# The second matrix products of both MLPs by two-by-two blocks in seven products, over pairs of chunks

## The chip, the cores and the metric

The program runs on one core of one Trainium2 chip. The time is the time on the device, in microseconds (us), from the start to the end of one execution; the kernel before took 1902.31 us (median of three runs, 1901.79 to 1906.84). Engines are named as in the profile: PE is the matrix engine, PEld its weight loads, DVE the vector engine, ACT the scalar engine, POOL the GpSimd engine, SP the engine that issues most DMAs.

## The reference, cut to what matters

The model is two trunk layers on 256 context tokens and 512 latent tokens of width 1024. Layer 0 mixes with differential attention, layer 1 with neighbourhood attention; behind each stands a dense MLP with a gate. Only the MLPs change here:

```
def squared_relu_mlp(h, w1, w2):
    return jnp.square(jax.nn.relu(h @ w1)) @ w2          # 1024 -> 4096 -> 1024
...
x = x + gate * squared_relu_mlp(modulate(rms_norm(x, g), shift, scale), w1, w2)
```

In layer 0 the MLP works on all 768 tokens, in layer 1 on the 512 latent tokens alone. Inputs and output are float32.

## The kernel before, in words

**Precision.** Every large product is made from float32 operands that are split in two: a rounded part, which ACT copies out as fp32r, and the rest, which POOL (weights, line 146) or DVE (activations) gets by subtraction. A product is then three matmuls (`PASSES`, line 59: high by high, high by low, low by high). So each weight tile of 128 by 1024 costs one ACT copy (line 145) and one POOL subtraction (line 146), and each PE product is threefold.

**The MLP** (`mlp`, line 810) goes over 16 chunks of 256 hidden units. `up(c)` makes the hidden chunk: two groups of weights are loaded and split, PE multiplies (line 830) into the PSUM tiles `D0` and `D1`, ACT takes the ReLU (lines 835 and 838), DVE squares (line 839), ACT and DVE split the result (lines 841 and 842) into tiles of tag `H`. `down` (line 856) multiplies a chunk with its two rows of `w2`: for each tile of 128 tokens and each half of 512 output columns six matmuls (line 865; two hidden halves, three passes) fill one PSUM tile, and DVE adds it to an accumulator in SBUF (line 876). The PSUM tile has the tag `A` for the left half and `B` for the right one; each tag has two buffers, so four groups of six can be in flight. `up` of the next chunk is issued ahead of `down` of this one. The last two chunks go through `down` together, straight onto the residual: before that `blend` (line 847) multiplies the accumulators by the gate (line 853, DVE) and adds them to the residual `xh` (line 854, POOL for the left, DVE for the right half), and then each PSUM tile is multiplied by the gate and added too (lines 871 and 872). In layer 0, `done0` passes each pair of finished token tiles on to the normalisation for layer 1.

**Buffers.** Raw weights land in `R` (two buffers), split weights in `W` (four buffers). The accumulators of layer 0 take four tiles `H`; the residual sits in `E` and `X` during the whole MLP.

**Order.** In the MLPs nothing is ordered by hand: a scheduler that builds the program fixes each engine's order ahead of time, and each engine then runs its own list in order, waiting on semaphores. Between the chunks of layer 0, `side` issues work for layer 1: a modulation chunk (line 257 on PE) and tables of position bias (line 594 on POOL).

## Time and profile before

| | |
|---|---|
| median of three runs | 1902.31 us |
| the profiled execution | 1902.15 us, of which the span from first to last instruction is 1899.6 us |
| granted clock of PE, mean over the span | 0.981 |
| PE busy | 1786.5 us (94%) |
| DVE busy | 1133.4 us (60%) |
| POOL busy | 812.6 us (43%) |
| MLP of layer 0 in the span | from about 550 to about 1138 us |
| MLP of layer 1 in the span | from about 1541 us to the end |

The page of the profile shows one execution. A busy PE is not PE at its peak, since matmuls are pipelined; how long a matmul takes in a row of matmuls is read from the distance of starts. In the time lines, an instruction of DVE or POOL that waits for access to the memory is shown as busy, not as idle: its duration grows.

### The profile page before, as it was taken

The numbers are of one execution on the slowest core, as the hardware profiler recorded it, in microseconds if no ns is written. First come the engines' busy times: TensorE is split into PE (matmuls) and PEld (weight loads), VectorE is DVE, ScalarE is ACT, GpSimd is POOL, SyncE is SP. The second block draws the span as 40 slices with busy tenths as digits, with TensorE's granted clock in tenths as the row PEclk, the third lists the DMA queues.
The fourth block names the chain that finished last, engine by engine and source line by source line (L and its number), as shares of the span: only waits on it lengthen the run. The fifth ranks groups of instructions, "written<-read, shape, count | busy, mean of one in ns | idle before, by whom it ended". The sixth has DMA issues, their size and how long they took to land.

```text
span 1899.6 us, 27132 instructions
## 1 busy us (share of the span) xinstructions
PE 1786.5 (94%) x10256; PEld 1563.8 (82%) x10256; DVE 1133.4 (60%) x2158; ACT 833.7 (44%) x1854; POOL 812.6 (43%) x688
## 2 busy tenths in 40 slices
PE   6989999996999999999999998999998989999998
PEld 5878888884789888888888977989897778888886
DVE  4588777885574343343334676777777664444446
ACT  4476767774342212221221245777676342323321
POOL 3755566653224333342432432433345444444443
PEclk9999999997999999999999998999999999999999
DMA  8122222224324443443432132122212323223232
GB/s 329 42 84 78 87 87 87 79 71 169 119 73 136 132 160 111 167 162 116 148 134 85 56 100 64 57 71 74 65 67 89 117 92 97 89 91 109 90 101 76
DMA packets 66499, 197.61 MB, mean 104 GB/s; under 512 B 8192, under 2 KB 23488, under 8 KB 60224
## 3 DMA queue, kind: packets, MB, share of 16 engines
q1 hardware_dynamic: 58608, 186.03, 29.4%
q10 hardware_dynamic: 7760, 9.85, 1.5%
q8 instruction: 80, 1.31, 0.3%
q14 instruction: 51, 0.42, 0.1%
HBM read 180.74 MB, written 15.11 MB: 103 GB/s over the span
## 4 chain that ended last, share of the span: by engine, by line
PE 75%; DVE 11%; ACT 6%; issue 4%; POOL 2%; DMA 2%; ACTq 0%; SPq 0%; POOLq 0%; DVEq 0%
PE PD L830 22%; PE PA L408 14%; PE PA L865 11%; PE PB L865 9%; PE PA L750 4%; PE PA L257 2%; PE PS L517 2%; PE PB L552 2%; PE PQ L398 1%; PE PS L656 1%; PE PB L701 1%; PE PB L541 1%; PE PB L686 1%; DVE Y L423 1%; ACT W L145 1%
## 5 line engine op out<-in xcount | busy, mean ns | idle before, releaser
L146 POOL TENSOR_TENSOR W<-R,W 128x1024 fp32r<-128x1024 f32 x142 | 351.3, 2485 | 540.6 <-ACT W L145 537.0
L830 PE MATMUL PD<-Q,W 128*128 128x384 f32 (+2 forms) x1992 | 396.0, 346 | 2.4 <-DVE Q L334 1.1
L830 PEld LDWEIGHTS PD<-Q,W 128*128 128x128 f32 x1992 | 345.7, 188 | 33.7 <-issue 8.6
L145 ACT ACTIVATE W<-R 128x1024 fp32r<-128x1024 f32 (+1 forms) x172 | 172.7, 1021 | 450.7 <-PE PA L865 193.6
L865 PE MATMUL PA<-W,H 128*128 128x512 f32 x1080 | 275.4, 393 | 4.6 <-POOL W L146 3.0
L865 PEld LDWEIGHTS PA<-W,H 128*128 128x128 f32 x1080 | 200.1, 188 | 51.3 <-issue 4.5
L839 DVE TENSOR_TENSOR N<-N 128x768 f32<-128x768 f32 (+1 forms) x64 | 66.9, 1046 | 279.2 <-ACT N L835 170.4
L865 PE MATMUL PB<-W,H 128*128 128x512 f32 x840 | 209.2, 391 | 0.0
L865 PEld LDWEIGHTS PB<-W,H 128*128 128x128 f32 x840 | 157.4, 188 | 33.4
L408 PE MATMUL PA<-W,Q 128*128 128x384 f32 (+1 forms) x1008 | 174.3, 325 | 0.4 <-DVE H L621 0.4
L408 PEld LDWEIGHTS PA<-W,Q 128*128 128x128 f32 x1008 | 158.6, 191 | 0.7 <-DVE H L621 0.7
L296 POOL TENSOR_TENSOR SQ<-SQ,half 128x4 f32<-128x4 f32 (+1 forms) x96 | 94.7, 988 | 128.9 <-DVE SQ L421 127.7
L842 DVE SCALAR_TENSOR_TENSOR H<-N,H 128x768 fp32r<-128x768 f32 (+1 forms) x64 | 97.9, 1532 | 25.7 <-ACT H L841 25.0
L408 PE MATMUL PA<-WB,H 128*128 128x384 f32 x576 | 110.9, 345 | 0.8 <-DVE Q L469 0.8
L750 PE MATMUL PA<-W,H 128*128 128x512 f32 x384 | 97.5, 404 | 7.9 <-ACT H L743 5.1
L408 PEld LDWEIGHTS PA<-WB,H 128*128 128x128 f32 x576 | 101.1, 192 | 1.8 <-DVE Q L469 1.1
L830 PE MATMUL PD<-H,W 128*128 128x512 f32 (+1 forms) x408 | 94.1, 378 | 2.4 <-DVE SA L290 2.0
L876 DVE TENSOR_TENSOR H<-PA,H 128x512 f32<-128x512 f32 x78 | 53.8, 690 | 69.7 <-PE PA L865 69.7
L750 PEld LDWEIGHTS PA<-W,H 128*128 128x128 f32 x384 | 71.9, 192 | 25.9 <-ACT H L743 5.4
L523 ACT ACTIVATE E<-PS,SA 128x768 f32<-128x768 f32 (+1 forms) x96 | 72.9, 760 | 36.5 <-DVE SA L522 33.6
L830 PEld LDWEIGHTS PD<-H,W 128*128 128x128 f32 x408 | 73.8, 188 | 18.0 <-DVE H L334 2.9
L517 PE MATMUL PS<-Q,Q 128*128 128x256 f32 (+1 forms) x320 | 70.2, 352 | 19.1 <-ACT Q L446 9.9
(210 smaller groups left out, 3052.6 us busy)
## 6 DMA issues: line engine op xcount, KB each, us to landing
R<-in_w_dram SPq DMA_DIRECT2D x128, 512.0 KB
M<-in_wmod_dram SPq DMA_DIRECT2D x48, 1024.0 KB
R<-in_wqa_dram SPq DMA_DIRECT2D x32, 384.0 KB
R<-in_wqb_dram SPq DMA_DIRECT2D x32, 384.0 KB
Y<-in_rpb_dram SPq DMA_DIRECT2D x48, 128.0 KB
bias<-Y SPq DMA_DIRECT2D x48, 128.0 KB
X<-bias SPq DMA_DIRECT2D x8, 768.0 KB
R<-in_woa_dram SPq DMA_DIRECT2D x8, 512.0 KB
```

The costliest lines, as they stand in the source:

```text
L145: high = nc.scalar.activation(w[:, 0, :n], raw, AF.Copy)
L146: low = (eng or nc.gpsimd).tensor_sub(w[:, 1, :n], raw, w[:, 0, :n].bitcast(F32))
L296: nc.gpsimd.tensor_tensor(r, ss, self.half[:, :n], op=ALU.pow)
L408: nc.tensor.matmul(acc[:, :n], hT[kt][:, x, P * i:P * i + P], w[kt // 2][:, y, o:o + n], start=(kt == 0 and p == 0), stop=(kt == KT - 1 an ...
L517: nc.tensor.matmul(s[:, c0:c1], q[:, m, P * i:P * i + P], k[:, m, c0:c1], start=p == 0, stop=p == 1)
L523: nc.scalar.activation(e[:, m, :nk], s, AF.Exp, bias=mx[:, 0:1], accum_out=sm[:, m:m + 1])
L750: nc.tensor.matmul(ps, oHL[h][:, x, c:c + P], w[h // 2][:, y, 512 * (h % 2):512 * (h % 2) + 512], start=(first and h == hs[0] and p == 0), ...
L830: nc.tensor.matmul(ps[:, at:at + b1 - b0], w[kt // 4][:, x, o:o + P], hT[kt][:, y, b0:b1], start=(kt == 0 and p == 0), stop=(kt == KT - 1 ...
L839: nc.vector.tensor_mul(r, r, r)
L842: nc.vector.scalar_tensor_tensor(u[:, 1, :], r, 1.0, u[:, 0, :].bitcast(F32), op0=ALU.mult, op1=ALU.subtract)
L865: nc.tensor.matmul(ps, hd[:, x, P * i - c0:P * i - c0 + P], w[f][:, y, 512 * n:512 * n + 512], start=(f == 0 and p == 0), stop=(f == len(h ...
L876: nc.vector.tensor_add(av, ps, av)
```

## The change

`mlp` gets two new arguments. With `blocks`, chunks 0 to 13 are taken in seven pairs. The two chunks of a pair and the two halves of the output columns cut `w2` into four blocks of 256 by 512 (B11, B12, B21, B22; first index the chunk, second the column half), and the two halves of the tokens cut the hidden values into four blocks. The eight block products of a pair become seven, each of a sum or difference of hidden blocks with a sum or difference of weight blocks (Strassen's scheme in Winograd's form). Since one intermediate sum enters three of the four results, there are five accumulators (`C11`, `C12`, `C21`, `C22`, `U`), and `blend` adds `U` to the last three once at the end. Chunks 14 and 15 go as before. Eight block products in one pair were 144 matmuls in layer 0 and 96 in layer 1; the seven are 126 and 84.

In detail:

- `raw_hidden` keeps the hidden values in float32, unsplit; ACT now squares them (it was DVE). The subtractions and additions of hidden blocks run on DVE, and `split` then splits each of the seven sums (ACT copy, DVE subtraction).
- `block` loads a weight block (128 by 2 by 512). Sums of blocks run on DVE, in place, 1024 elements per partition; each of the seven is split like any weight (ACT, POOL). The four blocks of a pair are loaded seven times in all, since `products_a` (two products) and `products_b` (five) load their own.
- `product` takes one PSUM tile for each tile of tokens and adds it to one or two accumulators. It sets the tag of the tile by a counter's parity; the counter moves by two for each tile, so all tiles of a product have the same tag.
- The order of a pair is: `up` of the pair's second chunk, two products, `up` of the next pair's first chunk, five products. The last pair has no next chunk.
- In layer 0 the fifth accumulator and the float32 hidden values take the tiles `E` and `X`. So the residual is written to DRAM (`x1`, twelve DMAs on the ACT queue) before the MLP, and read back in `blend`; the gates are loaded there too. Raw weight blocks land in the four buffers `N` in layer 0, and in layer 1 in `R`, which has four buffers there, shared with the raw weights of `up`.

The diff, cut to its core:

```
@@ mlp
-    def mlp(self, l, t0, xh, hT, tag, mid, done, side):
+    def mlp(self, l, t0, xh, hT, tag, mid, done, side, blocks=None, spilled=None):
...
+            if blocks:
+                nc.scalar.activation(r, r, AF.Square)
+            else:
+                nc.vector.tensor_mul(r, r, r)
+        def parts(u, src):
+            nc.scalar.activation(u[:, 0], src, AF.Copy)
+            nc.vector.scalar_tensor_tensor(u[:, 1], src, 1.0, u[:, 0].bitcast(F32), op0=ALU.mult, op1=ALU.subtract)
...
+        def raw_hidden(c):
+            r = self.sbt(r_tags[c % 3], [P, 2, ntok])
+            for f, ps in up(c):
+                relu2(c, ps, r[:, f, :])
+            return [r[:, :, 128 * nh * t:128 * nh * t + 128 * nh] for t in range(2)]
+        def block(c, n):
+            raw = self.sbt(b_tag, [P, 1024])
+            self.last["SP"] = nc.sync.dma_start(
+                raw.rearrange("p (f n) -> p f n", f=2),
+                a["w2"][l, 2 * c:2 * c + 2, :, 512 * n:512 * n + 512].rearrange("f p n -> p f n"))
+            return raw
...
+        def product(u, w, *sums):
+            for i in range(nh):
+                self.n += 1
+                ps = self.pst('AB'[self.n % 2])
+                for f in range(2):
+                    for p, (x, y) in enumerate(PASSES):
+                        nc.tensor.matmul(ps, u[:, x, f, P * i:P * i + P], w[:, y, 512 * f:512 * f + 512],
+                                         start=(f == 0 and p == 0), stop=(f == 1 and p == 2))
+                for q, sign in sums:
+                    av = piece(q * nh + i)
...
+                    elif sign > 0:
+                        nc.vector.tensor_add(av, ps, av)
+                    else:
+                        nc.vector.tensor_sub(av, av, ps)
+        def products_a(c, r1):
+            b11, b22, b12 = block(c, 0), block(c + 1, 1), block(c, 1)
+            w, u = self.wsplit(b11, 1024), split(r1[0])
+            nc.vector.tensor_sub(b22, b22, b12)
+            product(u, w, (C11, 1), (U, 1))
+            nc.vector.tensor_sub(r1[0], r1[0], r1[1])
+            w, u = self.wsplit(b22, 1024), split(r1[0])
+            product(u, w, (C21, 1), (C22, 1))
+        def products_b(c, r1, r2):
+            b22, b11, b21, b12 = block(c + 1, 1), block(c, 0), block(c + 1, 0), block(c, 1)
+            w, u = self.wsplit(b21, 1024), split(r2[0])
+            product(u, w, (C11, 1))
+            nc.vector.tensor_sub(b12, b12, b11)
+            nc.vector.tensor_add(r1[1], r1[1], r2[1])
+            w, u = self.wsplit(b12, 1024), split(r1[1])
+            product(u, w, (C12, 1), (C22, 1))
+            nc.vector.tensor_sub(b11, b22, b12)
+            nc.vector.tensor_sub(r1[0], r2[1], r1[0])
+            w, u = self.wsplit(b11, 1024), split(r1[0])
+            product(u, w, (U, 1))
+            nc.vector.tensor_sub(r1[1], r2[0], r1[0])
+            w, u = self.wsplit(b22, 1024), split(r1[1])
+            product(u, w, (C12, 1))
+            nc.vector.tensor_sub(b12, b11, b21)
+            w, u = self.wsplit(b12, 1024), split(r2[1])
+            product(u, w, (C21, -1))
         def blend():
+            if spilled is not None:
+                gate.update(self.load_gates(l, 1, (0, 1) if t0 == 0 else (0,)))
+                xu = [self.sbt('EX'[j % 2], [P, 3, 512]) for j in range((nx + 2) // 3)]
+                for j in range(nx):
+                    i, n = t0 + j // 2, j % 2
+                    xh[i, n] = xu[j // 3][:, j % 3, :]
+                    nc.sync.dma_start(xh[i, n], spilled[i][:, 512 * n:512 * n + 512])
...
+                        if t or n:
+                            nc.vector.tensor_add(av, piece(U * nh + k), av)
@@ mlp, the loop
+            r1 = raw_hidden(0)
+            for c in range(0, nc_ - 2, 2):
+                r2 = raw_hidden(c + 1)
+                side()
+                products_a(c, r1)
+                side()
+                if c + 2 < nc_ - 2:
+                    nxt = raw_hidden(c + 2)
+                side()
+                products_b(c, r1, r2)
+                side()
+                r1 = nxt
+            hid = hidden(nc_ - 2)
@@ project, end
+                if l == 0:
+                    for n in range(2):
+                        nc.scalar.dma_start(self.x1[i][:, 512 * n:512 * n + 512], xh[i, n])
@@ hybrid_block
-            b.mlp(0, 0, xh, hT2, 'HH', mid0, done0, sideB)
+            b.mlp(0, 0, xh, hT2, 'HH', mid0, done0, sideB, ('HHHHE', 'XEX', 'N'), b.x1)
...
+        b.open("right", R=2)
...
-            b.mlp(1, 2, xh1, hT3, 'QH', lambda: None, done1, lambda: None)
+            b.mlp(1, 2, xh1, hT3, 'QH', lambda: None, done1, lambda: None, ('QQQQ', 'NNN', 'R'))
```

In what follows the seven products of a pair are called a1, a2 and b1 to b5, in the order of the code, and the six matmuls that fill one PSUM tile a group. Line numbers from 843 on in rows of the change are those of the changed file: L843 is `up`, L903 the matmul of `product`, L911 and L913 its additions, L861 the splitting of a hidden block, L919 to L942 the sums of blocks, L964 and L965 `blend`.

**PE in the MLP of layer 0.** Before, a stretch of `down` (line 865; tiles `PA` and `PB`) with pieces of `up` (line 830) between:

```order
L830 MATMUL PD_8776<-Q_6233,W_8768 128x384
L865 MATMUL PB_8686<-W_8638,H_8276 128x512 x3
L865 MATMUL PB_8686<-W_8643,H_8331 128x512 x3
L865 MATMUL PB_8702<-W_8638,H_8276 128x512 x3
L865 MATMUL PB_8702<-W_8643,H_8331 128x512 x3
L865 MATMUL PA_8678<-W_8638,H_8276 128x512 x3
L865 MATMUL PA_8678<-W_8643,H_8331 128x512 x3
L830 MATMUL PD_8776<-Q_6233,W_8768 128x384 x2
L830 MATMUL PD_8776<-Q_6234,W_8768 128x384 x2
L865 MATMUL PA_8694<-W_8638,H_8276 128x512 x3
```

Now, the products b1, b2 and the start of b3 in a pair:

```order
L903 MATMUL PA_7790<-W_7784,H_7787 128x512 x6
L273 MATMUL PA_7750<-sel,T_7759 128x2 x2
L903 MATMUL PA_7798<-W_7784,H_7787 128x512 x6
L903 MATMUL PA_7806<-W_7784,H_7787 128x512 x6
L903 MATMUL PA_7822<-W_7816,H_7819 128x512 x6
L903 MATMUL PA_7831<-W_7816,H_7819 128x512 x6
L903 MATMUL PA_7840<-W_7816,H_7819 128x512 x6
L843 MATMUL PD_7980<-Q_6232,W_7972 128x384 x2
L843 MATMUL PD_8031<-Q_6232,W_7972 128x384 x2
L903 MATMUL PA_7857<-W_7851,H_7854 128x512 x6
L903 MATMUL PA_7865<-W_7851,H_7854 128x512 x6
```

Six groups stand one behind the other with nothing between them but two small matmuls, and all use the tag `A`; before, both tags were in use at once and `up` filled in between.

**DVE at the same kind of place.** Before, the additions of one chunk with what stands among them:

```order
L839 TENSOR_TENSOR N_9988<-N_9988 128x768
L876 TENSOR_TENSOR H_6662<-PA_10030,H_6662 128x512
L842 SCALAR_TENSOR_TENSOR H_9991<-N_9988,H_9991 128x768
L876 TENSOR_TENSOR H_6662<-PB_10038,H_6662 128x512
L876 TENSOR_TENSOR H_6663<-PB_10054,H_6663 128x512
L267 TENSOR_TENSOR T_10006<-PA_9994,T_10006 2x256
L876 TENSOR_TENSOR H_6662<-PA_10046,H_6662 128x512
L876 TENSOR_TENSOR H_6663<-PB_10070,H_6663 128x512
```

Now, from the last addition of b1 to the first of b3 (another pair than above, with the tag `B`):

```order
L911 TENSOR_TENSOR H_6675<-PB_8942,H_6675 128x512
L911 TENSOR_TENSOR H_6676<-PB_8958,H_6676 128x512
L911 TENSOR_TENSOR H_6678<-PB_8958,H_6678 128x512
L280 TENSOR_TENSOR mB<-PA_8888,bT 128x4
L861 SCALAR_TENSOR_TENSOR H_9052<-E_8540,H_9052 128x768
L911 TENSOR_TENSOR H_6676<-PB_8967,H_6676 128x512
L911 TENSOR_TENSOR H_6678<-PB_8967,H_6678 128x512
L919 TENSOR_TENSOR N_9244<-N_9244,N_9246 128x1024
L911 TENSOR_TENSOR H_6676<-PB_8976,H_6676 128x512
L911 TENSOR_TENSOR H_6678<-PB_8976,H_6678 128x512
L861 SCALAR_TENSOR_TENSOR H_9251<-X_8775,H_9251 128x768
L911 TENSOR_TENSOR E_6679<-PB_8993,E_6679 128x512
```

Between the additions that free the PSUM tiles of b2 and b3 there now stand operations with both inputs in SBUF (L861 and L919), one between each two groups.

**POOL at the end of layer 0's MLP.** Before, the additions of `blend` (line 854) stand ahead of and among the last four splits of `w2`:

```order
L854 TENSOR_TENSOR E_6167<-E_6167,H_6662 128x512 x2
L854 TENSOR_TENSOR X_6168<-X_6168,H_6663 128x512
L854 TENSOR_TENSOR E_6169<-E_6169,H_6664 128x512 x2
L146 TENSOR_TENSOR W_10754<-R_10752,W_10754 128x1024
L854 TENSOR_TENSOR X_6170<-X_6170,H_6665 128x512
L146 TENSOR_TENSOR W_10759<-R_10757,W_10759 128x1024
L146 TENSOR_TENSOR W_10764<-R_10762,W_10764 128x1024
L146 TENSOR_TENSOR W_10769<-R_10767,W_10769 128x1024
L146 TENSOR_TENSOR H_10772<-R_10773,H_10772 128x768
```

Now (L965 is `blend`):

```order
L146 TENSOR_TENSOR W_10898<-R_10896,W_10898 128x1024
L146 TENSOR_TENSOR W_10903<-R_10901,W_10903 128x1024
L146 TENSOR_TENSOR W_10908<-R_10906,W_10908 128x1024
L146 TENSOR_TENSOR W_10913<-R_10911,W_10913 128x1024
L965 TENSOR_TENSOR X_10848<-X_10848,H_6675 128x512
L965 TENSOR_TENSOR E_10849<-E_10849,H_6677 128x512 x2
L965 TENSOR_TENSOR X_10850<-X_10850,H_6677 128x512
L965 TENSOR_TENSOR E_10847<-E_10847,H_6675 128x512
L146 TENSOR_TENSOR H_10916<-R_10917,H_10916 128x768
L965 TENSOR_TENSOR E_10847<-E_10847,H_6675 128x512
```

All six additions of `blend` on POOL have moved behind the last split of `w2`, and those for the first tokens (`E_10847`) are the last of them.

78 lines of the change are left out of this document (50 added, 28 removed).

## The prediction

> **What bounds the kernel now.** I read the page's first part, then the busy times by stretches of time, then the chain of waits and the groups of the two MLPs, then the time lines of single periods.
>
> ```profile
> span 1899.6 us, 27132 instructions
> PE 1786.5 (94%) x10256; PEld 1563.8 (82%) x10256; DVE 1133.4 (60%) x2158; ACT 833.7 (44%) x1854; POOL 812.6 (43%) x688
> ...
> 438.00:550.00 112.00, 96.75 (x470) 75.77 (x471) 68.13 (x124) 41.66 (x96) 29.90 (x21) 0.90 0.31 103
> 640.00:1045.00 405.00, 405.00 (x2257) 348.91 (x2256) 155.08 (x206) 87.66 (x109) 143.35 (x84) 1.00 0.39 134
> 1595.00:1836.00 241.00, 241.00 (x1055) 197.69 (x1054) 109.47 (x132) 69.60 (x88) 105.21 (x44) 1.00 0.31 96
> ...
> 645.95 2.63 PE PD L830 x15
> 682.63 2.63 PE PD L830 x15
> ...
> 1595.12 9.90 PE PD L830 x43
> 1617.09 9.90 PE PD L830 x43
> ```
>
> In the steady part of both MLPs (640 to 1045 and 1595 to 1836 us; the columns behind the length are PE, PEld, DVE, ACT, POOL, the granted clock, the DMA share and GB/s) PE is busy without a break at clock 1.00, and the chain repeats every 36.68 us in layer 0 and 21.97 us in layer 1, one period for each chunk. DVE is busy for 38% and 45% there. So PE bounds the MLPs, and a matmul taken away is worth its place in the row. A chunk of layer 1 is 96 matmuls of 512 columns: 21.97 / 96 = 0.2288 us each, 1.37 us for a group of six.
>
> **What PE saves.** In layer 0 a pair drops from 144 to 126 matmuls of 512 columns, in layer 1 from 96 to 84. Seven pairs each: 126 × 0.2288 = 28.8 us and 84 × 0.2288 = 19.2 us, together **−48.0 us**. A pair would take 2 × 36.68 − 4.12 = 69.2 us in layer 0 and 43.93 − 2.75 = 41.2 us in layer 1.
>
> **What the other engines get.** The rows of layer 0, then pieces of time lines from both layers:
>
> ```profile
> L146 POOL TENSOR_TENSOR W<-R,W 128x1024 fp32r<-128x1024 f32 x44 | 108.5, 2478 | 260.5 <-ACT W L145 260.5
> L876 DVE TENSOR_TENSOR H<-PA,H 128x512 f32<-128x512 f32 x67 | 46.3, 691 | 65.0 <-PE PA L865 65.0
> L145 ACT ACTIVATE W<-R 128x1024 fp32r<-128x1024 f32 x44 | 45.4, 1055 | 238.4 <-PE PA L865 193.6 <-PE PD L830 44.8
> L842 DVE SCALAR_TENSOR_TENSOR H<-N,H 128x768 fp32r<-128x768 f32 x22 | 34.2, 1553 | 7.2 <-ACT H L841 7.2
> L835 ACT ACTIVATE N<-PD 128x768 f32<-128x768 f32 x22 | 17.9, 812 | 39.7 <-PE PD L830 39.7
> ...
> 799.18 1.44 POOL L594 TENSOR_TENSOR Y<-Y,C 128x256 f32<-128x256 f32 x2
> ...
> 803.16 0.96 DVE L842 SCALAR_TENSOR_TENSOR H<-N,H 128x768 fp32r<-128x768 f32 x1 [0.53 <-ACT H L841]
> 812.04 0.69 DVE L876 TENSOR_TENSOR H<-PA,H 128x512 f32<-128x512 f32 x1 [0.29 <-PE PA L865]
> 812.66 2.17 DVE L842 SCALAR_TENSOR_TENSOR H<-N,H 128x768 fp32r<-128x768 f32 x1
> 811.29 2.72 POOL L146 TENSOR_TENSOR W<-R,W 128x1024 fp32r<-128x1024 f32 x1 [0.36 <-ACT W L145]
> ...
> 1623.65 0.69 DVE L842 SCALAR_TENSOR_TENSOR H<-N,H 128x512 fp32r<-128x512 f32 x1 [0.70 <-ACT H L841]
> 1629.13 2.47 DVE L842 SCALAR_TENSOR_TENSOR H<-N,H 128x512 fp32r<-128x512 f32 x1
> 1631.52 0.68 DVE L876 TENSOR_TENSOR Q<-PB,Q 128x512 f32<-128x512 f32 x1
> 1632.12 0.67 DVE L876 TENSOR_TENSOR Q<-PA,Q 128x512 f32<-128x512 f32 x1
> 1628.65 2.40 POOL L146 TENSOR_TENSOR W<-R,W 128x1024 fp32r<-128x1024 f32 x1 [0.77 <-ACT W L145]
> ```
>
> The reader is to see that a DVE operation with both inputs in SBUF (L842) and a POOL operation never run at once. L842 takes 0.69 us with 512 columns when POOL rests; issued at 1629.13 beside a POOL split that ends at 1631.05, it ends at 1631.60, that is 0.55 us after POOL. With 768 columns it is 0.96 us alone and, at 812.66, ends 0.82 us after POOL's 814.01. An addition out of PSUM (L876) is untouched: 0.69 us in the middle of the POOL split at 811.29, and 0.60 us from start to start in a row. So I price a DVE operation on SBUF at 0.55 us (512), 0.81 (768) and, scaled, 1.08 (1024), **plus what is left of the POOL operation that it meets**, up to 2.40 us; and the additions queued behind it on DVE wait too.
>
> A pair now has 11 POOL splits instead of 8 (26.4 us), 15 such DVE operations (seven L861, four sums of weight blocks, four of hidden blocks) instead of 8, and ten additions out of PSUM for each three (layer 0) or two (layer 1) token tiles instead of eight: 30 in layer 0, 20 in layer 1. In layer 1 DVE has 20 × 0.6 + 11 × 0.55 + 4 × 1.08 = 22.4 us of its own, and POOL and DVE's SBUF operations together need 26.4 + 10.4 = 36.8 of 41.2 us one after the other. In layer 0 the same sum is 26.4 + 13.2 + 6 (eight bias tables of 0.72) = 46 of 69 us. ACT gets eleven copies of 1.06 us, four squares and seven copies of hidden blocks, some 20 to 25 us a pair; DMA gets three more loads of 0.5 MB (shares today 0.39 and 0.31). Both lie beside PE's work and I cost them at nothing; without that cover a copy would cost its 1.06 us and a load 3.6 us (below). Nothing is over the period, but in the products the additions come due every 1.37 us, and a product has only the **two PSUM buffers of one tag**: a group cannot start until the addition of the group two before it is done. DVE may be late by one group, no more.
>
> **Layer 0, a steady pair.** I walk from b2's first group (second stretch of the DVE order). It ends 1.37 us into b2; its two additions end at +2.8. L861 meets POOL, busy with b5's split until about +3.6 (its W buffer comes free as b1 ends, then 1.06 on ACT and 2.40), and ends at +4.4; the additions of group 2 end at +5.6; L919 meets the bias tables (0.7 us each) and ends at about +6.9, the additions of group 3 at +8.2. PE wants b3's first group at +4.8 and its second at +6.2, and gets them at +5.9 and +8.4: 2.2 us lost. Behind that, 15 to 18 matmuls of `up` between groups give DVE time. Bounds: 0 (DVE ahead) and 5 us (each SBUF operation meets a whole split). Nearest to the rows' mean wait (1553 − 960 = 0.6 us for L842) and doubled load, **+2.2 us × 6 pairs = +13**.
>
> **Layer 0, the last pair.** No next chunk stands between a and b: 13 groups (17.8 us) in a row, with 21 additions (12.6 us) and nine SBUF operations (7.6 us, and five splits to meet, about 1.5 us of waiting for six of the nine) in the same DVE list: 29 us. The tag's two buffers hold PE back to that: **+12** (5 to 18).
>
> **Layer 1, a steady pair.** The same walk gives 0.35 us at b3. Then `up`'s first matmuls wait for a raw weight, since its buffer is that of block B22, read last by b4's split.
>
> ```profile
> 1868.13 0.33 SPq L129 DMA_DIRECT2D R<-in_w_dram  x1
> 1871.70 1.06 ACT L145 ACTIVATE W<-R 128x1024 fp32r<-128x1024 f32 x1 [0.35 <-DMA R<-in_w_dram]
> ```
>
> A raw weight lands 3.57 us after its issue. b4's split can start only when `up` has ended (its W buffer), takes 1.06 (ACT) + 2.40 (POOL) and comes behind b3's: about +4.2 after b1 starts; + 3.57 + 1.06 = 8.8, while PE comes there at 7.2: 1.6 us. In pairs where POOL and not DVE goes first at a meeting in a, 1.5 us more; half of that. **+2.7 × 6 = +16** (0.5 to 5 each).
>
> **Layer 1, the last pair.** b1's split stands behind b3's on POOL and is done near 11.0 us; PE would come at 5.5. DVE then carries `blend`'s multiplications too: **+9** (4 to 13).
>
> **The ends.** In layer 0 `blend` was hidden under `up`. Now its last ten DVE operations and all six on POOL stand behind the last split:
>
> ```profile
> 1069.24 1.30 POOL L854 TENSOR_TENSOR E<-E,H 128x512 f32<-128x512 f32 x1 [0.63 <-DVE H L853]
> ...
> 1097.15 4.26 PE L865 MATMUL PA<-W,H 128*128 128x512 f32 x18
> 1101.66 0.73 PE L865 MATMUL PA<-W,H 128*128 128x512 f32 x2 [0.25 <-ACT H L841]
> 1105.06 8.47 PE L865 MATMUL PA<-W,H 128*128 128x512 f32 x36 [0.31 <-DVE T L871]
> 1106.78 1.85 POOL L146 TENSOR_TENSOR H<-R,H 128x768 fp32r<-128x768 f32 x1 [1.08 <-ACT H L145]
> ...
> 1873.36 1.95 PE L865 MATMUL PA<-W,H 128*128 128x512 f32 x6 [1.56 <-POOL W L146]
> 1876.14 1.51 PE L865 MATMUL PA<-W,H 128*128 128x512 f32 x4 [0.84 <-POOL W L146]
> ```
>
> Before, the fifth PSUM tile of the last product starts about 13.4 us after `up` ends (1097.15; 24 matmuls by 1105.06, 24 more at 0.2288). Now: the last split is done at 4.4 (0.8 ReLU and its start, 1.06 copy, 2.40), L861 at 5.2, then 10 × 0.55 + 6 × 1.3 = 13.3 us of `blend` one after the other, 18.5; then the first tokens' norm, whose power on POOL stands behind three splits of `wqb` (1.85 each): about 24. That is 11 later; since part may overlap, **+9** (0 to 14). On SP the reload of x into the tile that held `U` waits for `U`'s last use, and behind it stand three loads of `w2` and the gates; by the walk they land 3 us before the last `up` ends, hidden by its 16.5 us (24 × 4 matmuls of 384 columns). If that cover is gone, each costs 3.6. In layer 1 `blend` moves ahead of the last `up`'s end and shortens PE's waits for POOL of 1.56 + 0.84 us: **−2** (−4 to +1).
>
> Spilling x: twelve DMA issues on ACT in a stretch where PE is not full: **+1** (−1 to 4).
>
> By the Trainium skill ("TensorE: Matmul & The Clock Gate", What's actually happening) PE falls to half its clock after some 3.4 us of idleness and needs as long to come back; the row of 438 to 550 us, with its waits, has 0.90, which agrees. By that rule the two long waits above (last pair and end of layer 0) would cost 1.7 us each more, an estimate from that page; the sum goes without them.
>
> **Sum**, against the profiled execution's 1902.15 us: −48 + 13 + 12 + 16 + 9 + 9 − 2 + 1 = +10, so **1912 us**; this execution equals the median (1902.31) to 0.01%. All low ends give −48 + 0 + 5 + 3 + 4 + 0 − 4 − 1 = −41, all high ones +62.
>
> **The rivals.**
>
> *DVE keeps up in the steady pairs.* The scheduler's list already puts `up` behind most products; if the SBUF operations fall between splits, the 13 go, and layer 1 keeps 3 of 16: −48 + 3 + 12 + 9 + 9 − 2 + 1 = −16, **1886 us**. For it: DVE is under half busy today. Against: PE had four PSUM buffers and 24 additions then.
>
> *All is hidden*: −48, **1854 us**. Against it stand both last pairs, where nothing is left to cover with.
>
> *POOL and DVE become the bound of layer 1.* If every split is waited out by DVE without an addition beside it, a pair needs 22.4 + 26.4 = 48.8 us, 4.9 over the 43.93 before; it decides from 41.2 us on. Seven pairs: +34; layer 0 as forecast (−28.8 + 13 + 12 + 9 + 1 = +6): **1942 us**. Against: additions do run beside a split.
>
> *The work isn't less* is out: PE's list has 210 matmuls fewer, which is 126 + 84.
>
> **The numbers.** Forecast 0.50 (its own range 1897 to 1930), DVE keeps up 0.28, the bound moves 0.12, all hidden 0.05, and 0.05 for terms that cancel at no change. The measurement tells 0.3% (5.7 us) from nothing. Slower: 0.37 of the forecast and 0.12; within: 0.13, 0.04 of the rival that keeps up and 0.05; faster: 0.24 and 0.05. The range reaches to the second case and towards the fourth: 1884 to 1938.
>
> **What would show it.** Right: PE idle in each pair at b2 and b3, released by DVE's additions, L861 and L919 lasting 1.5 us and more; a pair near 71.4 us in layer 0 and 43.9 in layer 1; some 10 us lost in each last pair; the first tokens' `blend` late on POOL. Wrong: PE without a break in the products, periods near 69.2 and 41.2 us, or waits that POOL's splits or a DMA end and not DVE.

## The result, and the profile after

The changed kernel takes 1954.76 us (median of four runs, 1950.17 to 1958.5), the kernel before 1902.05 us beside it: 1.0272 times as long, with an interval of 1.026 to 1.0284. The direction of the forecast was right, its size was not: +52 us against +10, and the time lies outside the range of 1884 to 1938 us. The profiled execution has a span of 1954.1 us, against 1899.6 before.

The page of the kernel after, its first and fourth part:

```profile
span 1954.1 us, 27391 instructions
PE 1774.3 (91%) x10046; PEld 1534.1 (79%) x10046; DVE 1358.6 (70%) x2333; ACT 948.0 (49%) x2002; POOL 944.1 (48%) x730
PE 50%; DVE 20%; issue 12%; POOL 7%; ACT 6%; DMA 5%; ACTq 0%; SPq 0%; DVEq 0%; POOLq 0%
```

PE has 210 matmuls fewer and is busy for 12 us less, where 48 were counted. DVE, POOL and ACT now hold 33% of the chain that ended last (19% before).

**Where the time went.** Busy times by stretches, first of the kernel before, then of the kernel after; each time the MLP of layer 0 (from its first ReLU to the projection matmuls of layer 1 that follow a wait of 3.64 us on PE, 1153.91 us before and 1187.24 after) and that of layer 1 (from its first matmul to the end). The columns are length, PE, PEld, DVE, ACT, POOL, granted clock, DMA share, GB/s.

```profile
571.80:1153.90 582.10, 575.26 (x3162) 500.00 (x3160) 264.61 (x381) 144.73 (x207) 210.17 (x124) 1.00 0.37 123
1525.10:1899.60 374.50, 359.41 (x1605) 294.76 (x1603) 191.15 (x241) 106.30 (x141) 159.51 (x68) 0.99 0.30 94
```

```profile
572.80:1187.24 614.44, 568.23 (x3038) 482.75 (x3036) 384.10 (x477) 207.01 (x281) 272.99 (x145) 0.97 0.46 139
1557.70:1954.10 396.40, 355.53 (x1521) 283.61 (x1519) 294.81 (x320) 158.47 (x215) 228.85 (x89) 0.96 0.35 114
```

Layer 0 got 32.3 us longer, layer 1 21.9; together that is the 54.5 us of the span but for 0.3. PE's idle time (length less busy) went from 6.8 to 46.2 us in layer 0 and from 15.1 to 40.9 in layer 1. Its busy time fell by 7.0 and 3.9 us, though 28.8 and 19.2 us of matmuls are gone: what is left runs slower, and the clock column (0.97 and 0.96) says why in part. Summed over stretches of 3 us, PE busy times (1 − clock) is 11.6 us in layer 0 (0.0 before) and 11.7 in layer 1 (2.4 before): **21 us for the clock alone**. The remaining 16 us were not located one by one; waits that PE's busy column covers are among them, since a matmul's row (0.39 us) is longer than the 0.229 us to the next one's start.

**The steady pairs.** One DVE operation of each pair (L932), first and last start; the seven of layer 1, and those of layer 0 that include its first and its last pair:

```profile
L932 DVE TENSOR_TENSOR X<-X,E x3: 959/996/1646, 597.9 to 1043.7; 128x768 f32<-128x768 f32 x3
L932 DVE TENSOR_TENSOR N<-N,N x7: 1669/2014/2206, 1597.6 to 1872.3; 128x512 f32<-128x512 f32 x7
```

A pair takes (1043.7 − 597.9) / 6 = 74.3 us in layer 0, where 71.4 was forecast and 73.36 is what two chunks took before, and (1872.3 − 1597.6) / 6 = 45.8 in layer 1 (43.9 forecast, 43.94 before).

The largest wait of such a pair, on the time lines of DVE, POOL and PE in layer 1:

```profile
1610.69 1.70 DVE L861 SCALAR_TENSOR_TENSOR H<-N,H 128x512 fp32r<-128x512 f32 x1
1612.31 3.41 DVE L942 TENSOR_TENSOR R<-R,R 128x1024 f32<-128x1024 f32 x1
1615.65 1.28 DVE L911 TENSOR_TENSOR Q<-PB,Q 128x512 f32<-128x512 f32 x2
1608.45 11.86 POOL L146 TENSOR_TENSOR W<-R,W 128x1024 fp32r<-128x1024 f32 x4 [4.71 <-ACT W L145]
1616.47 7.48 PE L903 MATMUL PB<-W,H 128*128 128x512 f32 x24 [2.21 <-DVE Q L911]
```

POOL does four splits in a row. Beside them L861 takes 1.70 us and the last sum of weight blocks (L942) 3.41; the addition behind them in DVE's list starts at 1615.65, and PE, whose two buffers are full, gets its next group 2.21 us late. All six steady pairs have this wait (2.16 to 2.34 us).

**The end of layer 0** and the clock behind a wait:

```profile
1114.86 0.81 ACT L850 ACTIVATE N<-PD 128x768 f32<-128x768 f32 x1 [1.00 <-PE PD L843]
1133.76 6.50 PE L976 MATMUL PA<-W,H 128*128 128x512 f32 x15 [12.71 <-DVE T L981]
...
1130.00:1134.00 4.00, 0.24 (x1) 0.24 (x2) 4.00 (x5) 0.86 (x2) 1.95 (x2) 0.50 0.32 98
1134.00:1138.00 4.00, 4.00 (x10) 3.13 (x11) 4.00 (x3) 0.71 (x1) 3.94 (x2) 0.50 0.23 58
1138.00:1142.00 4.00, 4.00 (x15) 3.11 (x14) 2.50 (x6) 2.07 (x5) 1.02 (x3) 0.77 0.44 138
```

PE stands for 12.71 us in the last product; the first 4 us after that run at a clock of 0.50, the next 4 at 0.77.

### The profile page after: what moved, and what is told of

Read it like the earlier page. It is cut to its first block, busy times and chain, and to the rows that moved or that the text cites. A ratio compares the mean times of both kernels' runs of the same rounds, so it can differ in the third digit from the quotient of the medians.

```text
span 1954.1 us, 27391 instructions
## 1 busy us (share of the span) xinstructions
PE 1774.3 (91%) x10046; PEld 1534.1 (79%) x10046; DVE 1358.6 (70%) x2333; ACT 948.0 (49%) x2002; POOL 944.1 (48%) x730
## 4 chain that ended last, share of the span: by engine, by line
PE 50%; DVE 20%; issue 12%; POOL 7%; ACT 6%; DMA 5%; ACTq 0%; SPq 0%; DVEq 0%; POOLq 0%
PE PA L409 14%; PE PD L843 11%; POOL W L146 4%; PE PB L903 4%; PE PA L751 3%; PE PA L903 3%; DVE H L861 3%; PE PA L976 2%; PE PS L518 2%; DMA N<-in_w_dram 2%; DVE Q L911 2%; PE PB L553 2%; PE PQ L399 1%; PE PA L258 1%; PE PS L657 1%
## 5 line engine op out<-in xcount | busy, mean ns | idle before, releaser
L843 PE MATMUL PD<-Q,W 128*128 128x384 f32 (+2 forms) x1992 | 393.3, 346 | 10.6 <-DVE Q L335 5.0
L843 PEld LDWEIGHTS PD<-Q,W 128*128 128x128 f32 x1992 | 348.1, 190 | 41.6 <-ACT W L145 6.3
L145 ACT ACTIVATE W<-R 128x1024 fp32r<-128x1024 f32 (+1 forms) x165 | 168.3, 1022 | 265.3 <-issue 62.5
L903 PE MATMUL PB<-W,H 128*128 128x512 f32 x756 | 199.9, 407 | 22.0 <-DVE Q L911 9.3
L146 POOL TENSOR_TENSOR W<-N,W 128x1024 fp32r<-128x1024 f32 x49 | 120.7, 2464 | 197.0 <-ACT W L145 192.2
L903 PE MATMUL PA<-W,H 128*128 128x512 f32 x714 | 189.8, 411 | 24.5 <-DVE Q L911 15.4
L903 PEld LDWEIGHTS PB<-W,H 128*128 128x128 f32 x756 | 141.5, 193 | 64.4 <-issue 15.5
L903 PEld LDWEIGHTS PA<-W,H 128*128 128x128 f32 x714 | 137.9, 197 | 63.0 <-issue 12.5
L145 ACT ACTIVATE W<-N 128x1024 fp32r<-128x1024 f32 x49 | 52.0, 1060 | 167.2 <-PE PB L903 74.9
L751 PE MATMUL PA<-W,H 128*128 128x512 f32 x384 | 97.3, 403 | 8.4 <-ACT H L744 5.1
L861 DVE SCALAR_TENSOR_TENSOR H<-N,H 128x512 fp32r<-128x512 f32 (+1 forms) x57 | 79.4, 1408 | 35.0 <-ACT H L860 34.9
L843 PE MATMUL PD<-H,W 128*128 128x512 f32 (+1 forms) x408 | 98.0, 381 | 0.0
L751 PEld LDWEIGHTS PA<-W,H 128*128 128x128 f32 x384 | 71.9, 192 | 26.2 <-ACT H L744 5.4
L523 DVE TENSOR_REDUCE SA<-PS 128x1 f32<-128x768 f32 (+1 forms) x96 | 74.5, 776 | 21.9 <-PE PS L518 10.6
L518 PE MATMUL PS<-Q,Q 128*128 128x256 f32 (+1 forms) x320 | 70.5, 353 | 19.2 <-ACT Q L447 9.9
```

The source lines that it names most:

```text
L145: high = nc.scalar.activation(w[:, 0, :n], raw, AF.Copy)
L146: low = (eng or nc.gpsimd).tensor_sub(w[:, 1, :n], raw, w[:, 0, :n].bitcast(F32))
L518: nc.tensor.matmul(s[:, c0:c1], q[:, m, P * i:P * i + P], k[:, m, c0:c1], start=p == 0, stop=p == 1)
L523: nc.vector.tensor_reduce(mx, s, op=ALU.max, axis=AX, negate=True)
L751: nc.tensor.matmul(ps, oHL[h][:, x, c:c + P], w[h // 2][:, y, 512 * (h % 2):512 * (h % 2) + 512], start=(first and h == hs[0] and p == 0), ...
L843: nc.tensor.matmul(ps[:, at:at + b1 - b0], w[kt // 4][:, x, o:o + P], hT[kt][:, y, b0:b1], start=(kt == 0 and p == 0), stop=(kt == KT - 1 ...
```

## The experiments

The times of all runs, with a pair's period worked out as above from the same DVE operation; a pair's matmuls alone take 69.2 and 41.2 us by the forecast's sum. The columns "MLP" are the lengths of the stretches defined above. Pairs and stretches are of the profiled execution, the times are medians.

An edit also changes what the scheduler works with, and so it can change the order of the engines' lists. In the steady pairs the orders on PE and DVE are those of the kernel after only in the runs of one layer alone and of the early blend, and in layer 1 also in the runs without sums (but for the sums themselves) and on tag B. In all other runs a difference from the kernel after is that of the edit and of the new order together.

```
                                  median us   pair L0  pair L1   MLP L0   MLP L1
before                             1902         73.4     43.9     582.2    374.5
after                              1954.8       74.3     45.8     614.4    396.4
layer 0 alone                      1930.8       74.2      -       610.6    373.6
layer 1 alone                      1921.7        -       45.8     582.4    395.9
tags in turns (4 buffers)          1908.9       69.7     43.5     582.1    376.2
no splits on POOL                  1902.8       74.0     41.9     603.8    359.5
no sums of weight blocks           1924.7       73.2     42.8     606.8    373.1
neither splits nor sums            1886.7       72.4     41.8     590.2    356.0
products on tag B alone            1947.4       73.0     45.8     604.2    394.5
splits on DVE                      1933.7       74.4     43.4     617.2    372.9
early blend                        1945.2       74.2     45.9     605.5    394.6
tags, early blend                  1903.0       70.1     44.0     578.9    379.4
tags, early blend, up first        1914.5       70.5     43.5     587.6    382.8
tags, early blend, splits on DVE   1860.6       69.1     41.5     563.2    356.6
the same, blend's adds on DVE      1862.1       69.5     41.5     562.3    356.0
the same but up first              1869.7       69.3     41.2     569.1    355.6
before, splits on DVE              1887.8        -        -       580.1    367.2
```

**One layer at a time.** Is the loss of each layer its own? Layer 0 alone, with layer 1 as before:

```diff
-            b.mlp(1, 2, xh1, hT3, 'QH', ..., ('QQQQ', 'NNN', 'R'))
+            b.mlp(1, 2, xh1, hT3, 'QH', ...)
```

> The seven products in layer 0 alone, layer 1 as before the change. By the place of the loss in the trace (33 us in layer 0, 21 us in layer 1) and if the two layers do not act on each other: 1902 + 33 = 1935 us. If the loss of layer 1 hangs on layer 0 (its clock, its spills): below 1935 by what it does not bring.

And layer 1 alone, without the spill:

```diff
-            b.mlp(0, 0, xh, hT2, 'HH', mid0, done0, sideB, ('HHHHE', 'XEX', 'N'), b.x1)
+            b.mlp(0, 0, xh, hT2, 'HH', mid0, done0, sideB)
```

> The seven products in layer 1 alone, layer 0 as before the change, without the spill of x. By the same reading 1902 + 21 = 1923 us, with the same pair of 45.8 us in layer 1. A time near 1902 would say that layer 1's loss comes from what layer 0 leaves.

Measured: 1930.76 us (ratio 1.0164, 1.0144 to 1.0184) and 1921.65 us (1.0111, 1.0096 to 1.0126). The two losses, 29.5 and 20.4 us beside 1901.26, add up to 49.9 of the 53, which is the whole within the intervals: no action of one layer on the other is seen.

**The two buffers of one tag.**

```diff
-                self.n += 1
-                ps = self.pst('AB'[self.n % 2])
+                self.grp = getattr(self, 'grp', 0) + 1
+                ps = self.pst('AB'[self.grp % 2])
```

> Only the PSUM tag of a product's groups changes: they take turns between the two tags, so a product has four buffers and not two. If the two buffers of one tag are what turns DVE's lateness into PE's waits, most of the waits that an addition (L911) ends go: about 2 us for each steady pair of both layers, and 6 to 8 us for each last pair with the clock that they cost, so some 25 to 40 us less than the change, 1915 to 1930 us, and a pair of layer 1 near 43 us. If DVE and POOL are late by more than three groups because of the sheer amount of their work (rival), the waits only move by a group or two and less than 10 us go: 1945 us or more, a pair of layer 1 still over 45 us.

Measured: 1908.87 us (ratio 1.0044, 1.0029 to 1.0059), 46 us less, more than the theory asked for. PE's waits in its weight loads, over the six steady pairs of layer 0 (total us, times, longest), first of the kernel after, then with four buffers:

```profile
PEld PA L903 <- DVE H L911: 8.3, 7, 3.6
PEld PA L903 <- DVE E L911: 4.7, 4, 1.7
PEld PB L903 <- DVE H L911: 3.7, 6, 1.7
PEld PB L903 <- DVE E L911: 2.9, 4, 1.3
```

```profile
PEld PB L903 <- DVE H L911: 2.7, 3, 0.9
PEld PA L903 <- DVE H L911: 1.6, 3, 0.9
```

In layer 0 the pairs come to 69.7 us, next to PE's own 69.2. In layer 1 they come to 43.5 and half of the loss stays. That it is the buffers, and not only the new order, can be read from layer 1 at the place of the largest wait, shown above for the kernel after. With four buffers:

```profile
1622.45 2.89 DVE L861 SCALAR_TENSOR_TENSOR H<-N,H 128x512 fp32r<-128x512 f32 x1
1625.26 3.42 DVE L942 TENSOR_TENSOR R<-R,R 128x1024 f32<-128x1024 f32 x1
1628.61 0.68 DVE L911 TENSOR_TENSOR Q<-PA,Q 128x512 f32<-128x512 f32 x1
1624.36 1.52 PE L903 MATMUL PA<-W,H 128*128 128x512 f32 x6
1627.08 0.39 PE L903 MATMUL PA<-W,H 128*128 128x512 f32 x1
```

DVE is as late as it was: the first addition starts 4.25 us after the product's first group (1624.36 to 1628.61; in the kernel after 4.26 us, from 1611.39 to 1615.65). But PE goes on into a third and a fourth tile, and does not wait there.

**POOL's splits.** The low part as a second copy on ACT, in the MLPs up to the last pair:

```diff
+        if getattr(self, 'act_low', False) and eng is None and tile is None:
+            return nc.scalar.activation(w[:, 1, :n], raw, AF.Copy) and w
         low = (eng or nc.gpsimd).tensor_sub(w[:, 1, :n], raw, w[:, 0, :n].bitcast(F32))
```

> The change with its two buffers of one tag, but from the first chunk to the last pair the low part of every weight split is a second copy on ACT and not a subtraction on POOL. It leaves out the subtraction, so the low part is a copy of the high part. If DVE is late because its operations on SBUF wait for POOL's splits, L861 falls from 1.4 to 1.7 us to 0.6 to 1.0 and most of the steady waits go: 1910 to 1925 us. If the two buffers are short of DVE's own work even without POOL (rival): less than 15 us go, 1940 us or more.

Measured: 1902.77 us (ratio 0.9997, 0.9984 to 1.0011), with only two buffers, and 7 us below what the theory gave. Groups of DVE, both of layer 1, first of the kernel after, then without POOL's splits (lines are two further down there):

```profile
L861 DVE SCALAR_TENSOR_TENSOR H<-N,H 128x512 fp32r<-128x512 f32 x53 | 73.9, 1410 | 18.1 <-ACT H L860 17.9
L942 DVE TENSOR_TENSOR R<-R,R 128x1024 f32<-128x1024 f32 x7 | 23.9, 3416 | 0.0
```

```profile
L863 DVE SCALAR_TENSOR_TENSOR H<-N,H 128x512 fp32r<-128x512 f32 x53 | 38.7, 740 | 20.4 <-ACT H L862 20.3
L944 DVE TENSOR_TENSOR R<-R,R 128x1024 f32<-128x1024 f32 x7 | 8.5, 1217 | 1.5 <-ACT W L147 1.5
```

L861 falls from 1.41 to 0.74 us and the last sum from 3.42 to 1.22. Layer 1 shows the theory: its pairs fall to 41.9 us and its 2.2 us waits are gone. Layer 0 does not: its pairs stay at 74.0. There the same run shows another cause, on DVE and then on PE:

```profile
697.46 1.23 DVE L921 TENSOR_TENSOR N<-N,N 128x1024 f32<-128x1024 f32 x1 [2.45 <-DMA N<-in_w_dram]
698.60 2.48 DVE L913 TENSOR_TENSOR H<-PA,H 128x512 f32<-128x512 f32 x4
699.94 4.61 PE L905 MATMUL PA<-W,H 128*128 128x512 f32 x12 [2.93 <-DVE H L913]
```

The sum b22 −= b12 (line 919, here 921) stands in DVE's list and waits 2.45 us for its block to land; four additions stand behind it, and PE waits 2.93 us for the first two of them. The kernel after has no such wait at L919 in its steady pairs but one of 0.80 us, so this cause came in with the edit and its order.

**The sums of weight blocks.**

```diff
-            nc.vector.tensor_sub(b22, b22, b12)
...
-            nc.vector.tensor_sub(b12, b12, b11)
...
-            nc.vector.tensor_sub(b11, b22, b12)
...
-            nc.vector.tensor_sub(b12, b11, b21)
```

> The change with its two buffers, without the four sums of weight blocks of a pair (L919, L931, L935, L942); it leaves these sums out and multiplies blocks as they were loaded. They are four operations of 1.2 to 3.4 us each in the trace of the change. If they are the work that the additions wait behind, 20 to 35 us go: 1920 to 1935 us, and the wait of 2.2 us in each pair of layer 1 goes. If the additions are late by L861 and the hidden sums alone (rival): less than 10 us go, 1945 us or more.

Measured: 1924.68 us (ratio 1.0124, 1.0103 to 1.0145), 30 us less. In layer 1 the pair falls to 42.8 us: with the sums out of the list, PE waits about 1.1 us in every second pair where it was 2.2 in each; all other operations keep their order there. In layer 0 it falls by 1.1 us only.

**Why layer 0's additions are late.** Both edits at once (the diffs above together):

> The change with its two buffers, without POOL's splits (the low part is a copy of the high part) and without the four sums of weight blocks (the blocks are multiplied as loaded); both are left out, so the output is not kept. A pair of layer 0 is 74.0 us without the splits alone and 73.2 us without the sums alone, 69.2 by PE's work. If DVE's lateness in layer 0 has two sources that cover for each other, meetings with POOL and sums that stand in DVE's row waiting for their block's load, both gone give 69 to 71 us a pair. If two buffers are too few whatever DVE does (rival), the pair stays over 73 us.

Measured: 1886.74 us (ratio 0.9919, 0.9898 to 0.994), with a pair of (1023.7 − 589.6) / 6 = 72.4 us in layer 0, between the two theories. In two of these pairs PE waits for the modulation's weights, which is 1.2 us a pair:

```profile
840.99 1.72 PE L260 MATMUL PA<-M,silu 128*32 128x256 f32 x16 [4.63 <-DMA M<-in_wmod_dram]
915.04 1.07 PE L260 MATMUL PA<-M,silu 128*32 128x256 f32 x16 [2.48 <-DMA M<-in_wmod_dram]
```

Then the tag: a product on tag A shares its two buffers with the modulation.

```diff
-                ps = self.pst('AB'[self.n % 2])
+                ps = self.pst('B')
```

> The change with every product's PSUM tiles of the tag B: still two buffers for a product, but in layer 0 not those that the modulation's products for layer 1 (L258 to L273, tag A) take turns in. If in layer 0 the two buffers are often one, because a modulation tile holds the other, its pairs get 2 us shorter or more (72 us or less) and those of layer 1 stay at 45.8. If that sharing is not the cause (rival): 74 to 75 us a pair, 1950 us or more.

Measured: 1947.43 us (ratio 1.0237, 1.0209 to 1.0264); the pair of layer 0 falls by 1.3 us to (1030.4 − 592.7) / 6 = 73.0, that of layer 1 stays at 45.8 as it should. So leaving out sums and meetings took 1.9 us off layer 0's 5.1, leaving the shared tag 1.3 and four buffers 4.6, each with another order of the lists. These overlap, and no single source of DVE's lateness was found there; that the shared tag is a cause is argued and not shown. What is shown is that in the six pairs of layer 0 PE stands idle for 19.2 us with two buffers and for 2.1 with four.

**The splits on DVE.** The whole subtraction stays, on another engine:

```diff
+        if getattr(self, 'dve_low', False) and tile is None:
+            eng = nc.vector
```

> The change with its two buffers; in both MLPs the low part of every weight split is subtracted on DVE and not on POOL, so the output is kept. A pair gives DVE eleven more operations of about 1.1 us (34 of 41 us in layer 1), and nothing of these splits stands beside it on POOL. If what DVE loses is the waiting for POOL's 2.4 us splits, most of what the run without POOL's splits gained stays: 1908 to 1925 us. If it is the volume of DVE's own work between the additions (rival), 12 us more a pair make it worse: 1955 us or more.

Measured: 1933.72 us (ratio 1.0156, 1.0135 to 1.0177), between the two theories. Layer 1 gets 23.5 us shorter, of 36.9 without any splits: the meetings are gone, but DVE's own eleven splits cost 1.5 us a pair again. Layer 0 gets 2.8 us longer.

**The blend.**

```diff
+        if blocks:
+            blend()
         hid += hidden(nc_ - 1)
-        blend()
+        if not blocks:
+            blend()
```

> The blend (sums with U, gates, x) stands ahead of the last chunk's hidden values and not behind them. If the 12.7 us wait at the end of layer 0 and the half clock behind it come from DVE's and POOL's blend work that stands in the last product's way, 12 to 18 us go in layer 0 and next to nothing in layer 1: 1937 to 1943 us. If instead the reload of x on SP, which now stands ahead of the last chunk's weights and waits for U, holds up those weights (rival): the wait moves ahead of the last chunk, 1950 us or more.

Measured: 1945.22 us (ratio 1.0242, 1.0225 to 1.0259), 9.5 us less than the change and short of the 12 to 18 that were expected; in the profiled executions 8.9 in layer 0 and 1.8 in layer 1. PE's waits in the last product of layer 0 are shorter, but the blend now holds up the last chunk's own split and hidden values:

```profile
1118.04 0.51 PE L976 MATMUL PA<-W,H 128*128 128x512 f32 x1 [3.52 <-POOL W L146]
1122.81 3.36 PE L976 MATMUL PA<-W,H 128*128 128x512 f32 x7 [4.26 <-DVE H L861]
```

With the tags in turns as well:

> Both edits together: the two tags in turns and the blend ahead of the last chunk. If they act on different waits (46 us and 9.5 us apart), 1954.8 - 46 - 9.5 = 1899 us, level with before. If the blend's gain was made of waits that the tags have already removed (rival): 1906 us or more.

Measured: 1902.95 us (ratio 1.0001, 0.9988 to 1.0014), between the two, level with before. And with the up matmuls of the chunk before the last between the halves of the last pair:

```diff
                 if c + 2 < nc_ - 2:
                     nxt = raw_hidden(c + 2)
+                else:
+                    hid = hidden(nc_ - 2)
```

> As the one with both edits, and besides the up matmuls of the chunk before the last stand between the two halves of the last pair, as a next chunk's do in every other pair. If the last pairs wait because nothing stands between their halves (5.5 us of waits in layer 0 and 5.3 in layer 1 with the tags in turns, and half clock behind them), 8 to 12 us go: 1887 to 1891 us, faster than before the change. If that up is then missing as cover for the blend (rival), the waits only move to the end of each layer: 1897 us or more.

Measured: 1914.54 us (ratio 1.0067, 1.0046 to 1.0089), 11.6 us worse. In layer 0 the last pair now has a wait of 5.06 us for ACT's copy of a block, and the last product one of 8.13 for POOL's split, which stands behind the blend's additions there:

```profile
1049.63 0.79 PE L903 MATMUL PB<-W,H 128*128 128x512 f32 x1 [5.06 <-ACT W L145]
1110.35 13.66 PE L976 MATMUL PA<-W,H 128*128 128x512 f32 x46 [8.13 <-POOL W L146]
```

**All of it together.** The tags in turns, the early blend and the splits on DVE:

> The same splits on DVE, with the two tags in turns and the blend ahead of the last chunk. With four buffers and no split on POOL a pair should come near PE's floor (69.2 and 41.2 us): layer 1 some 12 to 15 us shorter than with both edits alone, layer 0 up to 10: 1878 to 1890 us, faster than before the change. If DVE at 34 of 41 us a pair cannot hold the additions in time (rival): 1900 us or more.

Measured: 1860.64 us (1858.69 to 1864.17), 0.9783 of before (0.9768 to 0.9797) and 0.952 of the change: 2.2% faster than the one and 4.8% than the other, and 17 us below what was expected. Its MLPs by stretches, and its pairs:

```profile
572.70:1135.84 563.14, 548.48 (x3036) 475.17 (x3034) 405.40 (x557) 207.51 (x281) 70.45 (x64) 1.00 0.48 152
1505.60:1862.20 356.60, 340.66 (x1519) 278.92 (x1517) 294.48 (x401) 159.00 (x214) 12.63 (x5) 0.99 0.39 126
...
L934 DVE TENSOR_TENSOR X<-X,E x3: 948/949/952, 596.5 to 1011.1; 128x768 f32<-128x768 f32 x3
L934 DVE TENSOR_TENSOR N<-N,N x7: 681/685/686, 1542.8 to 1791.9; 128x512 f32<-128x512 f32 x7
```

Pairs of 69.1 and 41.5 us are PE's own 69.2 and 41.2, and the clock is back at 1.00 and 0.99. The blend's remaining additions on DVE too:

> As that kernel, and the six additions of the blend that POOL did (ten in both layers) are on DVE too. If the blend's 1.7 to 2.3 us operations in layer 0 are meetings with POOL, the end of layer 0 (8.4 us of waits with both edits) loses 3 to 6 us more: 1874 to 1886 us. If the end waits for the last chunk's own split and hidden values (rival): no difference beyond 2 us.

Measured: 1862.05 us (ratio 0.9788, 0.9773 to 0.9803): no difference, as the rival had it. Yet the end of layer 0 did gain: PE's wait for a split (L148) in the last product is 3.33 us in the run before this one and 0.34 here. A new wait of 1.70 us for an addition in a steady pair takes part of it back. And the up matmuls first once more:

> The kernel with the tags in turns, the early blend and the splits on DVE (1860.6 us), and the up matmuls of the chunk before the last between the halves of the last pair, which cost 12 us where POOL did the splits. If that cost came from the last product's split behind the blend's additions on POOL (a wait of 8.1 us), it is gone, and the last pairs' waits (3 us and 5 us) with it: 1853 to 1860 us. If up is missing as cover behind the products (rival), the waits move to the ends: 1864 us or more.

Measured: 1869.65 us (ratio 0.9826, 0.9805 to 0.9847). The rival was right. The wait of 8.1 us is gone, so it was POOL's; the one in the last pair of layer 0 is the same to 0.01 us, and so POOL is not its cause:

```profile
1037.83 0.79 PE L905 MATMUL PB<-W,H 128*128 128x512 f32 x1 [5.06 <-ACT W L147]
1036.73 1.04 ACT L147 ACTIVATE W<-N 128x1024 fp32r<-128x1024 f32 x1
1036.00 0.83 ACT L862 ACTIVATE H<-X 128x768 fp32r<-128x768 f32 x1
```

ACT comes to the block's copy behind the last chunk but one's ReLU, squares and copies: the pair's own work stands behind the work that was put ahead of it.

**How much of this is the splits.** The kernel before with its splits on DVE:

> The kernel before, with the same splits of both MLPs on DVE. PE bounds its MLPs without a break, so nothing is to be had but the 2.4 us of waits for POOL at the end of layer 1: 1899 to 1903 us. If the kernel before, too, loses to POOL in a way the profile hides (rival): 1895 us or less, and the gain of the other runs is not the products'.

Measured: 1887.75 us (ratio 0.9925, 0.991 to 0.9939): the rival was right, 14.6 us. Not in the steady part, where PE was never idle: half of it lies in layer 1 (374.5 to 367.2 us), at its start and end. Its first 35 us, of the kernel before and then with the splits on DVE:

```profile
1525.10:1560.10 35.00, 27.70 (x162) 24.31 (x161) 23.90 (x43) 15.06 (x26) 14.58 (x7) 0.90 0.31 101
```

```profile
1520.50:1555.50 35.00, 31.41 (x179) 27.00 (x178) 22.81 (x50) 16.70 (x28) 0.55 (x1) 0.95 0.34 105
```

PE is busy for 3.7 us more and at a higher clock, and POOL's 14.6 us beside the norms are gone. The two profiled executions are 11.9 us apart: 7.3 in layer 1's MLP, 1.9 in layer 0's, and 2.7 outside of both, for which no cause was found. Against this kernel, run on the same chip, the products by blocks bring 1887.75 − 1860.64 = 27 us of the 48 that their matmuls are worth.

## Why the prediction was right or wrong

What PE saves (−48.0) was right: with four buffers and the splits on DVE the pairs come down to it. The price beside it was forecast at 58 us and measured at 102. By the prediction's own terms, with the periods and stretches above:

```
                              forecast    measured
layer 0, six steady pairs      +13         (74.3 - 69.2) x 6 = +30.6
layer 0, last pair, spill      +12 + 1     32.3 + 28.8 - 30.6 - 15.8 = +14.7
layer 0, end                   +9          72.4 - 56.6 = +15.8
layer 1, six steady pairs      +16         (45.8 - 41.2) x 6 = +27.5
layer 1, last pair             +9          21.9 + 19.2 - 27.5 + 1.8 = +15.4
layer 1, end                   -2          27.0 - 28.8 = -1.8
```

(The last pairs are what is left of each stretch, with its first chunk. The ends are counted from the last chunk's second ReLU: 1097.35 and 1870.78 us before, 1114.86 and 1927.13 after.)

- **The steady pairs of layer 0** are the term that failed most, 5.1 us a pair and not 2.2, just over its upper bound of 5. The releaser was right (L911), and so was the price of a meeting: the longest wait of these pairs follows an L919 that ends 1.08 us after the POOL split that it meets.

```profile
998.45 2.38 POOL L146 TENSOR_TENSOR W<-N,W 128x1024 fp32r<-128x1024 f32 x1 [4.46 <-ACT W L145]
998.75 3.16 DVE L919 TENSOR_TENSOR N<-N,N 128x1024 f32<-128x1024 f32 x1 [0.80 <-DMA N<-in_w_dram]
1003.16 4.61 PE L903 MATMUL PA<-W,H 128*128 128x512 f32 x12 [3.23 <-DVE H L911]
```

  The step that failed is "DVE may be late by one group, no more", walked at one place: DVE begins on time there and meets POOL at two operations, between b1 and b3. Of PE's eight waits of 1 us or more in the six pairs, six follow an L861 or a sum of weight blocks that took 2.5 to 3.3 us (0.95 and 1.2 alone), and two, of 1.20 us, follow ACT's copy for `up`, which the sum had at nothing. How the 5.1 us divide stays open: without POOL's splits the pair is only 0.3 us shorter, since in that run, with its own order, sums that wait for their load take the place of the meetings (five waits of PE of 1.5 to 2.9 us follow an L921 there).
- **The steady pairs of layer 1**, 4.6 and not 2.7. Here the mechanism was right: POOL's splits and DVE's operations on SBUF shut each other out, and with the splits gone 3.9 of the 4.6 us go. But the place was wrong. The walk put 0.35 us at b3 and the rest on a raw weight that comes late (3.0 us in all over the six pairs in the trace); the 2.2 us of each pair stand behind L861 and the last block sum, which meet four splits in a row. The walk let a meeting cost what is left of one split and then the list go free; with the next split right behind, L861 loses 1.0 us and L942 another 2.2.
- **The last pairs**: layer 0 nearly right (14.7 for 13), layer 1 too low (15.4 for 9, over its bound of 13). In both PE's waits end with additions behind DVE's operations on SBUF, as forecast for layer 0; for layer 1 (1.69, 3.82 and 2.30 us) the walk had b1's split on POOL in that place.
- **The end of layer 0**, 15.8 and not 9, over its bound of 14. The mechanism was right: the blend stands in the way of the last product. It was also costed at DVE's own 0.55 us for an operation; beside POOL most of them took 1.7 to 2.3.
- **The end of layer 1** was right to 0.2 us, and by its mechanism: PE's waits for POOL's splits behind the last ReLU, 1.56 and 0.84 us before, are one of 0.55 us after. The loads, costed at nothing, are not free where DVE's list waits for them, as the run without POOL's splits shows.
- **The clock** was left out of the sum; it is some 21 of the 44 us that were missed, by the sum over stretches above, and lies inside these terms. By the Trainium skill ("TensorE: Matmul & The Clock Gate", What's actually happening) two long waits would have cost 1.7 us each, an estimate from that page; measured were more dips than two, after shorter waits (below).

Of the rivals, "DVE keeps up" is out: DVE was the releaser in every pair. "POOL and DVE become the bound of layer 1" had the nearest time (1942) but not by its mechanism: a pair would take 48.8 us then, and takes 45.8. The shares that it works with do matter, as the run without splits shows.

## What to carry to other kernels

Before a matmul is traded for vector work, count the PSUM buffers of its products: here four instead of two took 46 of the 53 us back, since DVE's list, late behind a sum or a load, stops PE only when the buffers run out. POOL's splits beside DVE operations on two SBUF operands cost time on both engines here; with four buffers, giving all of them to DVE was cheaper (1903.0 to 1860.6 us), though DVE was the busier of the two. An edit that lets a scheduler order the lists anew is not an edit of one thing. And where small waits are added up, add the clock that they cost.

## What was not expected of the hardware

- **The clock falls after waits of about 2 us.** Two equal waits of layer 1 in the kernel after, 2.21 us (until 1616.47) and 2.19 us (until 1662.79), by stretches:

```profile
1616.00:1618.00 2.00, 1.53 (x6) 1.33 (x7) 0.93 (x2) 1.40 (x2) 2.00 (x2) 0.92 0.48 123
1618.00:1620.00 2.00, 2.00 (x6) 1.52 (x6) 1.62 (x3) 0.00 (x0) 2.00 (x1) 0.50 1.02 381
1620.00:1622.00 2.00, 2.00 (x8) 1.58 (x7) 1.92 (x3) 0.63 (x1) 0.31 (x1) 0.72 0.84 296
1664.00:1666.00 2.00, 1.89 (x9) 1.27 (x8) 1.55 (x3) 0.00 (x0) 2.00 (x2) 1.00 1.03 397
```

  After the first the clock is at 0.50 for some 3 us, after the second it stays at 1.00; two of the six such waits are followed by a dip (the other is the wait of 2.20 us until 1753.54, with 0.50 from 1755 to 1757). The Trainium skill ("TensorE: Matmul & The Clock Gate", What's actually happening) asks for some 3.4 us of idleness. Here 2.2 us were enough, though not each time.
- **Where POOL's splits stand in a row, a DVE operation on SBUF loses nearly a whole one.** In layer 1 the last block sum takes 3.42 us in each of seven pairs and 1.22 without the splits: 2.2 of a split's 2.40 us, every time. That POOL and DVE shut each other out agrees with the Trainium skill ("SBUF — State Buffer", Who interferes with whom).
- **The kernel before is 14.6 us faster with its splits on DVE**, though PE was busy without a break in the steady part of its MLPs.
